# Hybrid decoder layer: the last diagonal key block of each attention unit transposed and split in the bank of the second one, and the steps listed in a new order

## The chip, the cores and the metric

The kernel runs on one core of one Trainium2 chip. The metric is the device time of one execution in microseconds (us), lower is better. Engines are named as in the profile: PE is the matmul engine (PEld its weight loads), DVE the vector engine, ACT the scalar engine, POOL the general engine, SP the engine that issues most of the DMAs.

## The reference

One layer of a decoder works on 1024 rows of width 1024. A gated DeltaNet group and an attention group read the same normalised input; their outputs are projected together and added to the residual, then come an MLP of width 4096, an input embedding added under a gate, and a last norm. The change is in the attention group, which has eight heads and a causal softmax:

```python
def blocked_causal_attention(q, k, v):
    ...
    def block(args):
        q_blk, start = args
        s = jnp.einsum('bhqd,bhkd->bhqk', q_blk, k, preferred_element_type=jnp.float32) * scale
        q_idx = start + jnp.arange(Q_BLOCK)
        s = jnp.where(key_idx[None, :] <= q_idx[:, None], s, -jnp.inf)
        pr = jax.nn.softmax(s, axis=-1).astype(v.dtype)
        return jnp.einsum('bhqk,bhkd->bhqd', pr, v)
...
        y_mla = mla_mixer(c_q, c_kv, k_pe, positions, q_norm_w[i], w_q_b[i], kv_norm_w[i],
                          w_kv_b[i], mla_out_norm_w[i])
        h = h + jnp.concatenate([y_gdn, y_mla], axis=-1) @ w_out[i]
```

## The kernel before, in words

The kernel is one straight program. It is cut into 576 named steps, and a hand-written list, `STEPS`, gives the order in which their code is emitted. A scheduler then puts the instructions of each engine into one fixed order when the program is built; each engine works through its order and waits where an operand or a buffer is not there. SP issues its DMAs in such an order too, so that a DMA which waits for a buffer holds up those behind it.

Matrix operands that need full precision are kept as a rounded part ("hi") and a remainder ("lo"). `evac_split` makes both out of a PSUM bank: ACT casts the bank into hi (L179), then DVE subtracts hi from the bank into lo (L180).

Attention is worked off in 16 units: unit `u` is head `u // 2` and query half `g = u % 2`, that is 512 queries in four blocks of 128 (`i` = 0 to 3). The steps of a unit are:

- `s{u}_{i}` (`scores_block`): scores of one query block in PSUM (tile `ps_s`), the row maximum on DVE (`stat`), the exponential on ACT into `pn`.
- `v{u}_{kb}` (`values_part`): for the key block `kb` of 128 keys, PE transposes the blocks of `pn` (128x128 each) into one PSUM bank `pt_p`, of which there are two; `evac_split` makes `phl` of them; PE multiplies hi and lo with the values `V[..., kb]` and sums into the bank `po_a` (L1124, L1125), of which there is one. On the diagonal, `kb >= 4 * g`, only the query blocks that see the key block take part: key block `4g` has four query blocks (512 columns), `4g + 1` three (384), `4g + 2` two (256) and `4g + 3` one (128). A unit has `4g + 4` key blocks.
- `ve{u}` (`values_end`): ACT and DVE bring `po_a` to `oT` (L1134, L1135); the next unit's first product needs the bank.
- After each pair of heads `fa` and `fb` divide by the softmax sums (`rb`, on POOL or DVE, L1155), write `y_d`, and sum squares with 16 narrow matmuls on PE (`pss`, L1160).

Between them in the list stand steps of other parts: the DeltaNet outputs, head projections (`wn`, `wv1`, `vc`), the embedding (`plew` loads `wp0` and `wp1` and splits them: raw tiles `wp0r`, `wp1r`, halves `wp0h`, `wp1h`; `ei`, `eo` use them), and at the end the output projection: `wo0` to `wo7` load and split eight row blocks of the weight, `y0` to `y7` its input, `pa` (`po`, uses blocks 0 to 3) and `pb` (`po_o`, uses blocks 4 to 7) multiply, `h` loads the residual, `wu` the first weights of the MLP. Raw weights, `wp1r` and `rb` share pools of buffers with other tiles.

Of the kernel before, what the change touches and what calls it, by code (L numbers as in the profile page):

```python
# [64 lines left out]
STEPS = """
ldx0 ldm0 start ldx2 ldx1 ldx7 ldx3 ldm1 mixcol ldm2 nx0 nx1 ldm3 ldx5 tx0_3 nx2 nx3 tx0_7 ldx4 tx0_0 tx0_1 tx1_6
tx0_5 tx0_4 columns tx1_7 tx1_1 spm0 spm2 nx5 tx0_2 masks spm3 tx1_0 spm1 tx0_6 tx1_4 nx7 ldx6 tx1_3 tx1_2 tx1_5
misc2 nx4 nx6 tx2_5 misc0 misc1 tx2_0 la00 tx2_2 tx2_1 wl7 tx2_3 misc3 tx2_7 tx2_4 tx2_6 misc6 wl4 misc5 misc4 misc7
gates ip4 cv4 wl5 ssk0_0 ssk0_1 ip5 dec0 dec1 cv5 wl0 ssk1_1 wl6 ip7 ssk1_0 wl1 ip6 cv7 dec3 wl2 ssk3_0 dec2 cv6
ssk2_1 wl10 ssk2_0 gk1 ssk3_1 cvals ip1 rotary cv1 cunit ip0 gk0 cv0 ssq0_0 ssq0_1 uu1 ip2 gk2 uu2 gk3 uu0 uu3 wl3  # L70
sub sub0 ssq1_1 sub1 la11 sub2 sub3 sub4 sub5 sub6 sub7 sub8 sub9 xout ssq1_0 cv2 ssq2_1 wl8 wl9 ssq2_0 ip3 cv3 wl13
qout0 ip8 la10 cv8 rv0_0 rv0_1 kbd1_0 ga3 ga2 ssq3_0 qout1 wl11 ip9 cv9 kbd3_0 kbd2_0 tl0 kbd0_1 ga1 ga0 tm0 ip11
tn0 ip10 wl12 kbd1_1 rv1_0 tl1 tm1 kbd0_0 mw0 cv10 tl2 tl3 ip12 cv12 tn1 mw1 kbd3_1 kbd2_1 ssq3_1 rv2_0 rv1_1 tm2
tn2 cv11 ip13 cv13 rv3_1 tm3 tn3 mw2 mw3 rv3_0 mu0 sc0 rv2_1 mu3 mu1 wl15 mu2 sc1 sc2 sc3 wl14 ip15 qout2 ip14 cv14
la01 lt0_2 sc4 lt1_1 lt0_0 sc5 cv15 lt0_1 sc6 lt1_0 sc7 sc8 sc9 sc10 wv0 vb1 wpe qp0 vb0 qp1 sc11 vb3 rq8 vb2 lt1_2
rkey sc12 sc13 sc14 qout3 ol6 qp7 qr00 qp2 vb6 wn0 kn0_1 vb5 ol0 vb4 kn0_0 sc15 ol2 ol3 qn0_0 qp4 vb7 ol1 kp3 oa0
qp5 oa1 kp0 ob0 qp6 qp3 qn0_1 qr01 qr11 oa2 ro0_0 s0_1 qr10 s0_2 s0_3 ro0_1 s0_0 v0_0 v0_1 v0_2 s1_2 s1_0 s1_1 v0_3
ve0 s1_3 v1_0 v1_1 v1_2 v1_3 v1_4 kp1 s2_0 v1_5 kp2 v1_6 v1_7 ve1 ob1 ob2 s2_2 oa3 s2_1 ol4 oa4 ob3 s2_3 ob4 s3_1
ol5 s3_0 oa6 v2_0 s3_3 v2_1 v2_2 oa5 ob6 s3_2 v2_3 wn1 qn1_0 ro1_0 qn1_1 kn1_1 ve2 v3_0 v3_1 kn1_0 ro1_1 v3_2 v3_3
v3_4 s4_2 s4_1 fa0 ol7 s4_0 oa7 s5_2 s4_3 v3_5 v3_6 v3_7 ve3 v4_0 v4_1 v4_2 s5_1 fb0 s5_0 s6_2 s5_3 v4_3 ob5 s6_1  # L80
ve4 v5_0 kp5 s7_1 v5_1 v5_2 v5_3 v5_4 v5_5 v5_6 wv1 vc1 s6_3 ob7 ro2_0 s7_2 v5_7 s7_0 vc0 plew ei0 ei1 eo1 eo0 s6_0
h2 ve5 v6_0 v6_1 v6_2 wn2 kn2_0 v6_3 vc4 vc5 vc3 s7_3 vc7 ve6 v7_0 v7_1 v7_2 v7_3 qn2_0 vc6 vc2 v7_4 fa1 ei2 v7_5
qn2_1 kp4 s8_3 kn2_1 s8_1 eo2 ro2_1 v7_6 s8_2 s8_0 kp7 s9_3 s10_3 s9_1 s9_0 v7_7 ve7 v8_0 fb1 v8_1 v8_2 v8_3 s9_2
ve8 v9_0 v9_1 v9_2 v9_3 v9_4 ei3 s10_0 eo3 s10_2 s10_1 s11_1 s11_0 ei4 v9_5 v9_6 v9_7 ro3_0 ve9 s11_2 eo4 v10_0
v10_1 v10_2 v10_3 ve10 s11_3 ei5 ro3_1 eo5 wn3 qn3_0 kn3_0 v11_0 kn3_1 kp6 v11_1 v11_2 v11_3 v11_4 fa2 s12_2 qn3_1
ei6 s12_1 s12_0 v11_5 v11_6 v11_7 ei7 y0 ve11 s12_3 v12_0 v12_1 v12_2 v12_3 s13_3 eo6 ve12 s13_2 s13_1 eo7 fb2 s13_0
v13_0 v13_1 v13_2 s14_1 v13_3 v13_4 y2 v13_5 s14_3 v13_6 v13_7 ve13 s14_2 s14_0 v14_0 v14_1 y1 v14_2 v14_3 ve14 wo0
s15_0 s15_1 h6 s15_3 s15_2 v15_0 wo1 wo2 v15_1 wo3 y4 y5 y3 fa3 v15_2 v15_3 v15_4 v15_5 v15_6 h3 h4 pa4 y6 v15_7
ve15 fb3 wo4 h7 pa3 rsy h0 wo5 h5 wo6 pa0 y7 pa5 pa7 pa6 wo7 h1 wu0 pb3 pa2 pb2 nh2 nh3 pb0 nh0 pb7 pa1 uo0 pb1 nh1 th0_1
pb4 nh7 wu1 pb6 nh6 th0_0 th0_2 nh4 pb5 nh5 th0_3   th1_1 th1_0  th1_2  th1_3    # L90
 
"""
# [1530 lines left out]
```

## Time and profile before

| | |
|---|---|
| median of 3 runs | 1457.66 us (1456.11 to 1465.13) |
| profiled execution | 1459.25 us, span of its trace 1457.5 us |
| busy, share of the span | PE 95%, PEld 78%, DVE 69%, ACT 45%, POOL 21% |
| attention, 412 to 641 us of the trace | 229 us |
| rest of the output projection, 641 to 705 us | 64 us |

A busy share is the time in which an engine works on an instruction. Times in the rows below are microseconds from the start of the span, and the mean of one instruction is in nanoseconds. PEclk is the clock that was granted to PE as a share of its full speed.

### The profile page before, as it was taken

Reading aid. Unit: us, or ns where it says so; the run is one execution under the profiler, and the core shown is the slowest. Engines: PE = TensorE matmul, PEld = TensorE weight load, DVE = VectorE, ACT = ScalarE, POOL = GpSimd, SP = SyncE. Lnnn points to the kernel's source line nnn. Section 1 sums busy time; section 2 is a strip of 40 time slices with the busy share of each in tenths; the row PEclk is TensorE's granted clock in tenths of the full one; section 3 lists DMA queues with packets and bytes.
Section 4 is the critical chain, followed back from the end, with each engine's and each line's share of the span. In section 5 each row is a group of like instructions: output and inputs, shape, how many; then the busy total and the mean of one; then the engine's idle time right before and its main releaser. Section 6 shows DMA issues by size and latency. Waiting matters only on the chain.

```text
span 1457.5 us, 22314 instructions
## 1 busy us (share of the span) xinstructions
PE 1380.4 (95%) x8575; PEld 1130.7 (78%) x8575; DVE 1007.5 (69%) x1617; ACT 662.8 (45%) x1169; POOL 307.4 (21%) x417
## 2 busy tenths in 40 slices
PE   5999968999899999999989999999999999999897
PEld 4877847887677777888767888878887888888786
DVE  5567499545679687764697877778758775765464
ACT  6444210322357788842554544445534333333442
POOL 5412196321243511231510000000000000001410
...
GB/s 214 49 54 59 131 58 130 85 81 86 59 66 65 140 82 106 152 196 130 88 66 151 159 159 159 159 137 125 214 333 230 159 96 126 183 116 134 170 44 58
DMA packets 133590, 182.54 MB, mean 125 GB/s; under 512 B 38896, under 2 KB 88188, under 8 KB 133484
## 3 DMA queue, kind: packets, MB, share of 16 engines
...
q10 hardware_dynamic: 160, 0.27, 0.0%
HBM read 122.99 MB, written 58.10 MB: 124 GB/s over the span
## 4 chain that ended last, share of the span: by engine, by line
PE 47%; DVE 11%; DMA 8%; ACT 6%; issue 3%; POOL 1%; SPq 1%; DVEq 0%; POOLq 0%; ACTq 0%
DMA i_d<-D 4%; PE dmo L214 3%; PE dme L214 3%; PE dmo L215 3%; PE dme L215 3%; PE dme L213 3%; PE dmo L213 3%; DMA dar<-i_d 2%; PE pgt L215 2%; PE pgt L213 2%; PE pgt L214 2%; PE um L215 2%; PE um L214 2%; PE um L213 2%; PE pt_p L1119 1%
## 5 line engine op out<-in xcount | busy, mean ns | idle before, releaser
L1495 DVE TENSOR_TENSOR dal<-dar,dah 128x1024 fp32r<-128x1024 f32 x56 | 68.5, 1224 | 74.4 <-issue 32.1
L1544 POOL DMA_DIRECT2D rowg<-in_ple_gate_norm_w x1 | 0.6, 644 | 505.4 <-DVE dbs L1499 505.4
L214 PE MATMUL dme<-dbl,dah 128*128 128x512 f32 x256 | 99.7, 390 | 0.0
L215 PE MATMUL dme<-dbh,dal 128*128 128x512 f32 x256 | 99.4, 390 | 0.0
L213 PE MATMUL dme<-dbh,dah 128*128 128x512 f32 x256 | 99.2, 390 | 0.0
L1494 ACT CAST dah<-dar 128x1024 fp32r<-128x1024 f32 x56 | 58.8, 1050 | 62.0 <-DMA dar<-i_d 59.5
L1501 ACT CAST dbh<-dbs 128x1024 fp32r<-128x1024 f32 x40 | 42.1, 1053 | 90.1 <-DVE dbs L1499 45.6
L214 PE MATMUL dmo<-dbl,dah 128*128 128x512 f32 x192 | 74.4, 390 | 1.8 <-DVE dbl L1502 1.8
L215 PE MATMUL dmo<-dbh,dal 128*128 128x512 f32 x192 | 74.3, 390 | 0.0
L213 PE MATMUL dmo<-dbh,dah 128*128 128x512 f32 x192 | 72.8, 390 | 0.0
L180 DVE TENSOR_TENSOR phl<-pt_p,phl 128x512 fp32r<-128x512 f32 (+1 forms) x96 | 51.8, 550 | 17.8 <-ACT phl L179 16.8
L1098 DVE TENSOR_REDUCE stat<-ps_s 128x1 f32<-128x384 f32 (+5 forms) x96 | 51.5, 551 | 16.4 <-PE ps_s L1097 9.7
L213 PEld LDWEIGHTS dme<-dbh,dah 128*128 128x128 f32 x256 | 48.1, 188 | 10.0
L214 PEld LDWEIGHTS dme<-dbl,dah 128*128 128x128 f32 x256 | 48.1, 188 | 9.9
L215 PEld LDWEIGHTS dme<-dbh,dal 128*128 128x128 f32 x256 | 48.1, 188 | 9.9
L213 PE MATMUL um<-uc,t52h 128*128 128x512 f32 x128 | 51.4, 402 | 3.5 <-DVE Cb L1420 2.7
L179 ACT CAST phl<-pt_p 128x512 fp32r<-128x512 f32 (+1 forms) x96 | 44.5, 480 | 21.9 <-PE pt_p L1119 19.5
L1502 DVE TENSOR_TENSOR dbl<-dbs,dbh 128x1024 fp32r<-128x1024 f32 x40 | 48.9, 1222 | 6.7 <-ACT dbh L1501 6.4
L214 PE MATMUL um<-uc,t52h 128*128 128x512 f32 x128 | 50.8, 397 | 2.6 <-DVE uc L1282 2.6
L214 PE MATMUL um<-uc,t34h 128*128 128x512 f32 x128 | 50.7, 396 | 0.7 <-DVE uc L1282 0.7
L213 PE MATMUL um<-uc,t34h 128*128 128x512 f32 x128 | 50.9, 398 | 0.0
L215 PE MATMUL um<-uc,t34l 128*128 128x512 f32 x128 | 50.4, 393 | 0.0
...
## 6 DMA issues: line engine op xcount, KB each, us to landing
...
```

The lines of the kernel that those rows point to most:

```text
L179: nc.scalar.copy(out=hi, in_=src)
L180: nc.vector.tensor_tensor(out=lo, in0=src, in1=f(hi), op=ALU.subtract)
L213: nc.tensor.matmul(outp, ah, bh, start=first, stop=False)
L214: nc.tensor.matmul(outp, ah, bl, start=False, stop=False)
L215: nc.tensor.matmul(outp, al, bh, start=False, stop=last)
L1098: nc.vector.tensor_reduce(out=st[:, c:c + 1], in_=ps[c], axis=AX.X, op=ALU.max, negate=True)
L1119: nc.tensor.transpose(pt[:, i * P:(i + 1) * P], pn_view(u, i)[:, kb * P:(kb + 1) * P], ident)
L1494: nc.scalar.copy(out=ah, in_=raw)
L1495: nc.vector.tensor_tensor(out=al, in0=raw, in1=f(ah), op=ALU.subtract)
L1501: nc.scalar.copy(out=bh, in_=s_)
L1502: nc.vector.tensor_tensor(out=bl, in0=s_, in1=f(bh), op=ALU.subtract)
L1544: nc.gpsimd.dma_start(out=rowg, in_=ple_gate_norm_w[0].partition_broadcast(P))
```

## The change: what it does

In `values_part`, the one 128x128 block of the last key block (`kb + 2`, query block 3) is transposed into the bank of the second diagonal key block, ahead of its three. The bank is then 512 columns wide instead of 384, and is cast and subtracted once. After the two products of the second key block (384 columns) follow the two of the last one (128 columns, with its own values, L1141 and L1142). The step of the last key block goes, so that a unit has `4g + 3` value steps, and the third diagonal key block (256 columns) comes last; `ve{u}` waits for that one. PE has the same transposes and products as before; ACT has 16 casts of 128 columns less, DVE 16 subtractions of 128 columns less, and 16 casts and 16 subtractions grow from 384 to 512 columns. `STEPS` is also listed in another order from attention on. In the build the two kernels' engine orders are alike up to the start of attention, and again from the MLP's first product on; between them they differ. Line numbers of after are 9 higher up to the scores, and 17 higher behind `values_part`.

```diff
-ve0 s1_3 v1_0 v1_1 v1_2 v1_3 v1_4 kp1 s2_0 v1_5 kp2 v1_6 v1_7 ve1 ob1 ob2 s2_2 oa3 s2_1 ol4 oa4 ob3 s2_3 ob4 s3_1
...
+s1_0 s1_1 ve0 s1_3 v1_0 v1_1 v1_2 v1_3 v1_4 kp1 s2_0 v1_5 kp2 v1_6 ve1 ob1
...
-        for i in range(i0, 4):
-            nc.tensor.transpose(pt[:, i * P:(i + 1) * P], pn_view(u, i)[:, kb * P:(kb + 1) * P], ident)
-        cs = slice(i0 * P, 512)
+
+        parts = [(kb, i) for i in range(i0, 4)]
+        if i0 == 1:
+            parts.insert(0, (kb + 2, 3))
+        for j, (b, i) in enumerate(parts):
+            nc.tensor.transpose(pt[:, j * P:(j + 1) * P], pn_view(u, i)[:, b * P:(b + 1) * P], ident)
+        n = len(parts) * P
         ph, pl = hl(slot("phl", "phl", F32R))
-        evac_split(pt[:, cs], ph[:, cs], pl[:, cs])
-        vt = V[hh // 4, kb][:, hh % 4 * P:(hh % 4 + 1) * P]
-        nc.tensor.matmul(po[:, cs], vt, ph[:, cs], start=(kb == 0), stop=False)
-        nc.tensor.matmul(po[:, cs], vt, pl[:, cs], start=False, stop=(kb == nkb - 1))
+        evac_split(pt[:, :n], ph[:, :n], pl[:, :n])
+        vt = [V[hh // 4, b][:, hh % 4 * P:(hh % 4 + 1) * P] for b in (kb, kb + 2)[:1 + (i0 == 1)]]
+        cs, m = slice(i0 * P, 512), i0 == 1
+        nc.tensor.matmul(po[:, cs], vt[0], ph[:, m * P:n], start=(kb == 0), stop=False)
+        nc.tensor.matmul(po[:, cs], vt[0], pl[:, m * P:n], start=False, stop=(kb == nkb - 2))
+        if m:
+            nc.tensor.matmul(po[:, 384:512], vt[1], ph[:, 0:P], start=False, stop=False)
+            nc.tensor.matmul(po[:, 384:512], vt[1], pl[:, 0:P], start=False, stop=False)
...
-        for kb in range(4 * g + 4):
-            step(f"v{u}_{kb}", *(f"s{u}_{i}" for i in range(4)), f"v{'bc'[hh // 4]}{kb}", *([f"v{u}_{kb - 1}"] if kb else []),
+        for kb in range(4 * g + 3):
+            step(f"v{u}_{kb}", *(f"s{u}_{i}" for i in range(4)), f"v{'bc'[hh // 4]}{kb}", *([f"v{'bc'[hh // 4]}{kb + 2}"] if kb == 4 * g + 1 else []), *([f"v{u}_{kb - 1}"] if kb else []),
                  *([f"ve{u - 1}"] if u and not kb else []))(lambda u=u, kb=kb: values_part(u, kb))
-        step(f"ve{u}", f"v{u}_{4 * g + 3}")(lambda u=u: values_end(u))
+        step(f"ve{u}", f"v{u}_{4 * g + 2}")(lambda u=u: values_end(u))
```

The first place is PE at the end of unit 1 (head 0, second half), before: the products of its second, third and last diagonal key block; `pav` is DeltaNet work, `pn2a` the next unit.

```order
L1124 MATMUL po_a<-phl,V_3927 128x384
L1119 MATMUL pt_p<-ident,pn_4308 128x128
L1119 MATMUL pt_p<-ident,pn_4366 128x128
L1125 MATMUL po_a<-phl,V_3927 128x384
L1119 MATMUL pt_p<-ident,pn_4366 128x128
L885 MATMUL pav<-Uv_3092,A_3970 64x64 x16
L1124 MATMUL po_a<-phl,V_3899 128x256
L1125 MATMUL po_a<-phl,V_3899 128x256
L1124 MATMUL po_a<-phl,V_3899 128x128
L1119 MATMUL pt_p<-ident,pn2a 128x128 x3
L1125 MATMUL po_a<-phl,V_3899 128x128
```

The same place after:

```order
L1138 MATMUL po_a<-phl,V_3927 128x384
L1132 MATMUL pt_p<-ident,pn_4311 128x128
L1132 MATMUL pt_p<-ident,pn_4362 128x128
L1139 MATMUL po_a<-phl,V_3927 128x384
L1141 MATMUL po_a<-phl,V_3899 128x128
L1142 MATMUL po_a<-phl,V_3899 128x128
L1132 MATMUL pt_p<-ident,pn2a 128x128 x3
L894 MATMUL pav<-Uv_3092,A_3970 64x64 x12
L1138 MATMUL po_a<-phl,V_3899 128x256
L894 MATMUL pav<-Uv_3092,A_3970 64x64 x4
L1139 MATMUL po_a<-phl,V_3899 128x256
```

The narrow products moved ahead of the 256-column ones, and the unit's last product is one bank earlier.

The second place is the load of the embedding weights in the middle of attention. SP before:

```order
L1156 DMA y_d<-oT_4363 128x1024
L198 DMA wp0r<-in_w_ple_proj 128x1024
L198 DMA wp1r<-in_w_ple_proj 128x1024
L906 DMA y_d<-ot_4650 128x4x128
L979 DMA wv1r<-in_w_kv_b 128x4x64
```

SP after:

```order
L988 DMA wv1r<-in_w_kv_b 128x4x64
L207 DMA wp0r<-in_w_ple_proj 128x1024
L1173 DMA y_d<-oT_4359 128x1024
L207 DMA wp1r<-in_w_ple_proj 128x1024
L915 DMA y_d<-ot_4553 128x4x128
```

The loads of `wv1r` and `wp0r` moved ahead of the write of `oT`. On ACT the casts of these weights stand between casts of value blocks, before:

```order
L179 CAST phl<-pt_p 128x512
L192 CAST wp0h<-wp0r 128x1024
L179 CAST phl<-pt_p 128x512
L179 CAST phl<-pt_p 128x384
L192 CAST wp1h<-wp1r 128x1024
L179 CAST phl<-pt_p 128x256
L192 CAST wv_5315<-wv1r 128x256
```

ACT after:

```order
L201 CAST wp0h<-wp0r 128x1024
L188 CAST phl<-pt_p 128x512
L898 ACTIVATE ot_4979<-ot_4979 128x512
L1114 ACTIVATE pn6a,sums_110<-ps_s,stat 128x128
L188 CAST phl<-pt_p 128x512
L1008 CAST V_5266<-pv 128x2x64 x2
L188 CAST phl<-pt_p 128x256
L1047 ACTIVATE qh_5325<-pt_qp 32x512
L1151 COPY oT_5186<-po_a 64x512
L201 CAST wp1h<-wp1r 128x1024
```

The cast of `wp1h` moved behind the unit's last value block and its `oT` copy.

The third place is SP near the end of attention, around the last unit's `oT`. Before:

```order
L198 DMA wo5r<-in_w_out 128x1024
L1269 DMA h_7079<-in_x 128x1024
L1150 DMA rb_6921<-r_d 64x1024 x2
L1269 DMA h_7071<-in_x 128x1024
L198 DMA wo6r<-in_w_out 128x1024
L1231 DMA yr_7003<-y_d 128x1024
L1156 DMA y_d<-oT_6527 128x1024
L1231 DMA yr_7115<-y_d 128x1024
L198 DMA wo7r<-in_w_out 128x1024
L1269 DMA h_7213<-in_x 128x1024
L1351 DMA wu_7215<-in_w_up 128x4x256
L1351 DMA wu_7216<-in_w_up 128x4x256
```

After:

```order
L207 DMA wo6r<-in_w_out 128x1024
L1368 DMA wu_7030<-in_w_up 128x4x256
L1368 DMA wu_7031<-in_w_up 128x4x256
L1167 DMA rb_6853<-r_d 64x1024 x2
L1286 DMA h_6954<-in_x 128x1024
L1248 DMA yr_6956<-y_d 128x1024
L1173 DMA y_d<-oT_6475 128x1024
L1248 DMA yr_7075<-y_d 128x1024
L207 DMA wo7r<-in_w_out 128x1024
L1286 DMA h_7117<-in_x 128x1024
L207 DMA wo5r<-in_w_out 128x1024
```

The load of `wo5r` moved from far ahead of the write of `oT` to behind `wo7r`, and the two loads of `wu` moved ahead of `rb`.

## Rows read from the trace of the kernel before

**Rows 1.** Stretches: bounds, length, busy us and count per engine, PEclk, DMA share, GB/s.

```profile
412.00:641.00 229.00, 218.21 (x1561) 177.16 (x1560) 180.94 (x353) 173.04 (x451) 68.93 (x100) 0.99 0.38 124
...
641.00:705.00 64.00, 64.00 (x295) 53.26 (x294) 33.08 (x46) 17.73 (x26) 12.97 (x15) 1.00 0.25 91
705.00:745.00 40.00, 33.74 (x160) 26.78 (x159) 29.53 (x35) 26.52 (x47) 25.48 (x22) 0.87 0.24 79
```

**Rows 2.** Waits of PE, 412 to 641: waiting, releaser, total, times, longest.

```profile
PE po_a L1124 <- ACT phl L179: 2.2, 3, 1.1
...
PE po_a L1125 <- DVE phl L180: 0.9, 2, 0.7
```

**Rows 3.** Waits of ACT, the same stretch.

```profile
ACT phl L179 <- PE pt_p L1119: 18.6, 16, 5.2
...
ACT oT L1134 <- PE po_a L1125: 3.0, 3, 1.3
```

**Rows 4.** Groups by shape, ACT, 412 to 642: busy us, mean ns, idle before.

```profile
L179 ACT CAST phl<-pt_p 128x512 fp32r<-128x512 f32 x48 | 27.4, 586 | 9.9 <-PE pt_p L1119 9.4
...
L179 ACT CAST phl<-pt_p 128x384 fp32r<-128x384 f32 x16 | 7.7, 482 | 1.7 <-PE pt_p L1119 1.5
...
L179 ACT CAST phl<-pt_p 128x128 fp32r<-128x128 f32 x16 | 4.3, 266 | 1.2 <-PE pt_p L1119 1.2
```

**Rows 5.** Groups by shape, DVE, the same stretch.

```profile
L180 DVE TENSOR_TENSOR phl<-pt_p,phl 128x512 fp32r<-128x512 f32 x48 | 32.6, 682 | 5.5 <-ACT phl L179 4.9
...
L180 DVE TENSOR_TENSOR phl<-pt_p,phl 128x384 fp32r<-128x384 f32 x16 | 8.8, 550 | 2.3 <-ACT phl L179 2.2
...
L180 DVE TENSOR_TENSOR phl<-pt_p,phl 128x128 fp32r<-128x128 f32 x16 | 4.6, 286 | 2.0 <-ACT phl L179 1.7
```

**Rows 6.** Timeline of ACT around 490: start, length, instruction, idle before.

```profile
484.49 1.07 ACT L179 CAST phl<-pt_p 128x512 fp32r<-128x512 f32 x2
...
491.28 1.05 ACT L192 CAST wp0h<-wp0r 128x1024 fp32r<-128x1024 f32 x1 [1.01 <-DMA wp0r<-in_w_ple_proj]
...
494.87 1.04 ACT L192 CAST wp1h<-wp1r 128x1024 fp32r<-128x1024 f32 x1 [1.68 <-DMA wp1r<-in_w_ple_proj]
```

**Rows 7.** Groups by shape, PE, 412 to 642: the 128-column product.

```profile
L1124 PE MATMUL po_a<-phl,V 128*128 128x128 f32 x15 | 4.0, 269 | 0.0
```

**Rows 8.** Timeline of PE around 490.

```profile
492.86 0.49 PE L1124 MATMUL po_a<-phl,V 128*128 128x512 f32 x1 [0.63 <-ACT phl L179]
...
496.23 0.39 PE L1124 MATMUL po_a<-phl,V 128*128 128x256 f32 x1 [1.14 <-ACT phl L179]
```

**Rows 9.** Timeline of SP's DMA issues around 490.

```profile
487.11 0.42 SPq L198 DMA_DIRECT2D wp0r<-in_w_ple_proj  x1
490.08 0.33 SPq L198 DMA_DIRECT2D wp1r<-in_w_ple_proj  x1
```

**Rows 10.** Timeline of PE after the last value product.

```profile
645.53 0.28 PE L1125 MATMUL po_a<-phl,V 128*128 128x128 f32 x1
...
657.75 1.84 PE L1160 MATMUL pss<-ones,rb 128*128 128x1 f32 x16
```

**Rows 11.** Timeline of SP's DMA issues, same place.

```profile
655.46 0.37 SPq L198 DMA_DIRECT2D wo7r<-in_w_out  x1
...
656.40 1.15 SPq L1351 DMA_DIRECT2D wu<-in_w_up  x2
```

**Rows 12.** Timeline of ACT, same place.

```profile
652.36 1.06 ACT L1157 ACTIVATE rb<-oT 128x1024 f32<-128x1024 f32 x1 [4.86 <-POOL oT L1155]
...
660.26 1.05 ACT L192 CAST wo7h<-wo7r 128x1024 fp32r<-128x1024 f32 x1
```

**Rows 13.** Timeline of DVE, same place.

```profile
645.95 1.22 DVE L193 TENSOR_TENSOR wo5l<-wo5r,wo5h 128x1024 fp32r<-128x1024 f32 x1
```

**Rows 14.** Timeline of POOL, same place.

```profile
647.58 2.40 POOL L193 TENSOR_TENSOR wo6l<-wo6r,wo6h 128x1024 fp32r<-128x1024 f32 x1 [19.84 <-ACT wo6h L192]
```

**Rows 15.** Stretch 600 to 605, columns as in Rows 1.

```profile
600.00:605.00 5.00, 5.00 (x25) 4.37 (x25) 2.33 (x7) 3.41 (x10) 2.36 (x1) 0.68 0.47 151
```

More of the change, by code (lines that the diff above doesn't have):

```diff
@@ L65 @@
 STEPS = """
[L66 to L75, printed above, removed]
@@ L76 @@
-rkey sc12 sc13 sc14 qout3 ol6 qp7 qr00 qp2 vb6 wn0 kn0_1 vb5 ol0 vb4 kn0_0 sc15 ol2 ol3 qn0_0 qp4 vb7 ol1 kp3 oa0
-qp5 oa1 kp0 ob0 qp6 qp3 qn0_1 qr01 qr11 oa2 ro0_0 s0_1 qr10 s0_2 s0_3 ro0_1 s0_0 v0_0 v0_1 v0_2 s1_2 s1_0 s1_1 v0_3
-ve0 s1_3 v1_0 v1_1 v1_2 v1_3 v1_4 kp1 s2_0 v1_5 kp2 v1_6 v1_7 ve1 ob1 ob2 s2_2 oa3 s2_1 ol4 oa4 ob3 s2_3 ob4 s3_1
-ol5 s3_0 oa6 v2_0 s3_3 v2_1 v2_2 oa5 ob6 s3_2 v2_3 wn1 qn1_0 ro1_0 qn1_1 kn1_1 ve2 v3_0 v3_1 kn1_0 ro1_1 v3_2 v3_3
-v3_4 s4_2 s4_1 fa0 ol7 s4_0 oa7 s5_2 s4_3 v3_5 v3_6 v3_7 ve3 v4_0 v4_1 v4_2 s5_1 fb0 s5_0 s6_2 s5_3 v4_3 ob5 s6_1
@@ L81 @@
[L81 to L90, printed above, removed]
+ldx0 ldm0 start ldx2 ldx1 ldx7 ldx3 ldm1 mixcol ldm2 nx0 nx1 ldm3 ldx5 tx0_3 nx2
@@ new lines @@
+nx3 tx0_7 ldx4 tx0_0 tx0_1 tx1_6 tx0_5 tx0_4 columns tx1_7 tx1_1 spm0 spm2 nx5 tx0_2 masks
+spm3 tx1_0 spm1 tx0_6 tx1_4 nx7 ldx6 tx1_3 tx1_2 tx1_5 misc2 nx4 nx6 tx2_5 misc0 misc1
+tx2_0 la00 tx2_2 tx2_1 wl7 tx2_3 misc3 tx2_7 tx2_4 tx2_6 misc6 wl4 misc5 misc4 misc7 gates
+ip4 cv4 wl5 ssk0_0 ssk0_1 ip5 dec0 dec1 cv5 wl0 ssk1_1 wl6 ip7 ssk1_0 wl1 ip6
+cv7 dec3 wl2 ssk3_0 dec2 cv6 ssk2_1 wl10 ssk2_0 gk1 ssk3_1 cvals ip1 rotary cv1 cunit
+ip0 gk0 cv0 ssq0_0 ssq0_1 uu1 ip2 gk2 uu2 gk3 uu0 uu3 wl3 sub sub0 ssq1_1
@@ new lines @@
+sub1 la11 sub2 sub3 sub4 sub5 sub6 sub7 sub8 sub9 xout ssq1_0 cv2 ssq2_1 wl8 wl9
+ssq2_0 ip3 cv3 wl13 qout0 ip8 la10 cv8 rv0_0 rv0_1 kbd1_0 ga3 ga2 ssq3_0 qout1 wl11
+ip9 cv9 kbd3_0 kbd2_0 tl0 kbd0_1 ga1 ga0 tm0 ip11 tn0 ip10 wl12 kbd1_1 rv1_0 tl1
+tm1 kbd0_0 mw0 cv10 tl2 tl3 ip12 cv12 tn1 mw1 kbd3_1 kbd2_1 ssq3_1 rv2_0 rv1_1 tm2
+tn2 cv11 ip13 cv13 rv3_1 tm3 tn3 mw2 mw3 rv3_0 mu0 sc0 rv2_1 mu3 mu1 wl15
+mu2 sc1 sc2 sc3 wl14 ip15 qout2 ip14 cv14 la01 lt0_2 sc4 lt1_1 lt0_0 sc5 cv15
+lt0_1 sc6 lt1_0 sc7 sc8 sc9 sc10 wv0 vb1 wpe qp0 vb0 qp1 sc11 vb3 rq8
@@ new lines @@
+vb2 lt1_2 rkey sc12 sc13 sc14 qout3 ol6 qp7 qr00 qp2 vb6 wn0 kn0_1 vb5 ol0
+vb4 kn0_0 sc15 ol2 ol3 qn0_0 qp4 vb7 ol1 kp3 oa0 qp5 oa1 kp0 qp6 ob0
+qp3 qr01 qn0_1 ro0_0 oa2 qr11 s0_1 qr10 s0_2 s0_3 ro0_1 s0_0 v0_0 v0_1 v0_2 s1_2
+s1_0 s1_1 ve0 s1_3 v1_0 v1_1 v1_2 v1_3 v1_4 kp1 s2_0 v1_5 kp2 v1_6 ve1 ob1
+ob2 s2_2 oa3 s2_1 ol4 ol5 oa4 ob3 s2_3 ob4 s3_1 s3_0 v2_0 oa6 s3_3 v2_1
+oa5 ob6 s3_2 wn1 v2_2 kn1_1 ve2 qn1_0 ro1_0 qn1_1 v3_0 v3_1 kn1_0 ro1_1 v3_2 v3_3
+v3_4 s4_2 s4_1 fa0 ol7 s4_0 v3_5 oa7 s5_2 s4_3 v3_6 ve3 s5_1 v4_0 v4_1 v4_2
@@ new lines @@
+fb0 s5_0 s5_3 ob5 ve4 s6_1 s7_1 v5_0 kp5 v5_1 v5_2 wv1 s6_2 vc1 s6_3 v5_3
+v5_4 v5_5 v5_6 ro2_0 s7_2 vc0 plew s7_0 ob7 ei0 ei1 eo1 eo0 ve5 s6_0 v6_0
+v6_1 wn2 kn2_0 h2 vc4 vc5 vc3 s7_3 vc7 v6_2 ve6 v7_0 v7_1 v7_2 v7_3 qn2_0
+vc6 vc2 v7_4 qn2_1 kp4 fa1 ei2 v7_5 s8_3 kn2_1 s8_1 eo2 ro2_1 v7_6 s8_2 s8_0
+kp7 ei5 s9_3 s10_3 s9_1 s9_0 ve7 v8_0 fb1 v8_1 v8_2 s9_2 ve8 v9_0 v9_1 v9_2
+v9_3 v9_4 ei3 s10_1 s11_0 s11_1 ei4 v9_5 v9_6 ro3_0 ve9 s11_2 s10_0 eo3 s10_2 eo4
+v10_0 v10_1 v10_2 s11_3 ve10 eo5 wn3 ro3_1 v11_0 v11_1 qn3_0 kp6 kn3_0 s12_2 qn3_1 v11_2
@@ new lines @@
+kn3_1 v11_3 v11_4 fa2 ei6 s12_1 ei7 y0 v11_5 s12_0 v11_6 ve11 s12_3 v12_0 v12_1 v12_2
+s13_3 eo6 ve12 s13_2 s13_1 eo7 fb2 s13_0 v13_0 v13_1 v13_2 s14_1 v13_3 s14_3 v13_4 s14_0
+y2 v13_5 v13_6 ve13 s14_2 v14_0 y1 v14_1 v14_2 ve14 wo0 s15_0 s15_1 h6 s15_3 s15_2
+wo1 wo2 v15_0 y4 v15_1 wo3 y3 fa3 y5 wo4 v15_2 v15_3 h7 v15_4 h3 h4
+pa4 v15_5 v15_6 h0 y6 pa7 pa6 ve15 h5 wo6 wu0 fb3 pa0 y7 pa5 wo7
+h1 rsy pa3 wo5 pb3 pa2 pb2 pb0 nh2 pa1 nh3 nh0 pb1 pb7 nh1 uo0
+th0_1 pb4 nh7 nh4 wu1 pb6 nh6 th0_0 th0_2 pb5 th0_3 nh5 th1_1 th1_0 th1_2 th1_3
```

## The prediction

> **What bounds the kernel now.** I read the busy time by stretch first. Between 412 and 641 us, which is attention, PE is busy for 218.21 of 229.00 us, DVE for 180.94 (79%) and ACT for 173.04 (76%) [rows 1]. The reader is to see that PE bounds even this stretch, and that 10.8 us is all that PE has there in idle time. From 641 to 705 us PE is busy without a gap, 64.00 of 64.00; from 705 to 745 it lacks 6.3 us [rows 1], in the hand-over to the MLP, whose first products come when the last norms are transposed. Next I read what PE waits for in attention: 2.2 us in three waits for the cast of a value block and 0.9 us in two for its subtraction [rows 2]. The rest of the 10.8 us is split over many small waits for exponentials, projections and `oT`. The other engines wait for PE much longer: ACT waits 18.6 us for transposes before it can cast [rows 3]. So work taken off ACT or DVE is worth what PE waits for it, which is 3.1 us of the 10.8, and not its own length.
>
> **The change, part by part.** PE does the same transposes, products and columns, so its busy time has no term.
>
> *The merge.* For each unit a cast of 384 columns and one of 128 become one of 512: 482 + 266 - 586 = 162 ns less on ACT, by 16 units 2.6 us [rows 4]. The subtractions give 550 + 286 - 682 = 154 ns, 2.5 us on DVE [rows 5]. These are upper ends, because neighbours overlap: two casts of 512 columns take 1.07 us together where twice 586 is 1.17 [rows 6], so a dropped instruction frees some 0.06 to 0.16 us, 0.9 to 2.6 us in all. This lies beside PE's work. On the other side the first product of the merged block waits for a cast that is 104 ns longer (586 - 482) and a subtraction that is 132 ns longer (682 - 550): 0.236 us by 16 is 3.8 us, if PE stood waiting at each of them. The 384-column blocks are hidden now, and so are the 128-column ones, whose first product has an idle time of 0.0 over 15 units [rows 7]; the round trip that goes from the end of each unit was paid by PE nowhere that the profile shows. What can come of it is that ACT's copy of `oT`, which waits 3.0 us for the last product in three places [rows 3], is reached a bank earlier, and that the two busiest helpers are 1% less loaded. Between -2.6 and +3.8 us I take -1.0: it is nearest to the freed time after overlap (0.9), and the lengthening is covered by the product stream in between, as the 0.0 shows.
>
> The profile shows ACT at 76% and DVE at 79%, neither full, with PE waiting for both at times [rows 1, 2]. The Trainium skill (Perfetto Trace Analysis, section Optimizing Scalar/DVE Operations) says that grouping into larger operations helps where the engine is saturated, and that where it isn't and yet causes bubbles on other engines, breaking instructions up may let work finish sooner. By that rule the merge goes the wrong way; the term would be up to +3.8 instead of -1.0. It is the first rival below. The same section puts the fixed cost of an operation on PSUM at about 51 ns on ACT and 125 ns on DVE; by it the merge would free an estimated 0.8 and 2.0 us, inside the span from the rows.
>
> *The order around the embedding weights.* This is where PE's longest waits for a cast are. SP issues `wp0r` at 487.11, behind the write of `oT`, and `wp1r` only at 490.08 [rows 9]. ACT's order has both casts in the middle of value blocks: it stands idle for 1.01 us before `wp0h` and 1.68 before `wp1h` [rows 6], and PE then waits 0.63 us at 492.86 and 1.14 us at 496.23 for casts of value blocks queued behind them [rows 8]. After, `wp0r` is issued ahead of the write, and `wp1h`'s cast stands behind the unit's last block and its `oT` copy. The two waits have no reason left: 1.77 us. I take -2.0, since the subtraction behind a late cast is late too, with ends 0 and -2.7 (1.01 + 1.68, all of ACT's idling). At nothing it stands if the load of `wp1r`, which still waits for a buffer, lands later than the cast's new place; behind that cast is queued the next unit's first value block.
>
> *The rest of the order in attention.* Every score, value and projection step shifts by a few places. The same kinds of work are left, with the same buffers; new small waits replace old ones. PE's idle time without the above two places is about 8.8 us (10.8 - 2.0); one unit end less per round trip takes a little of it. I take -1.0, between -5 and +6. The upper end is some six waits of the longest kind seen (1.14 us) [rows 8].
>
> *The end of attention.* From 641 to 705 us PE never waits [rows 1], so nothing can be won, only lost. Let E be the end of the last value product, 645.53 + 0.28 = 645.8 [rows 10]. Before, POOL did `wo6l` for 2.40 us ahead of the last `oT` [rows 14]; the change casts `wo6h` before that unit ends, and `oT` with all behind it comes 2.4 us sooner after E. Two things run against PE. First, `pss` needs the squares of `oT`: 652.36 + 1.06 - 2.4 = 651.0, E + 5.2 [rows 12]; 43 products stand between E and `pss`, at 64.00 / 295 = 0.217 us each [rows 1], so PE reaches it at E + 9.3. Margin 4.1 us. Second, `wo5r` is now issued two rows behind `wo7r`, where `wu` was: 656.40 - 2.4 = 654.0 [rows 11]. `wo7r` was cast 4.8 us after its issue (660.26 - 655.46) [rows 11, 12], so `wo5r` lands by 658.8. Its cast stands behind `wo7h`: 660.26 + 1.05 - 2.4 = 658.9, end 660.0; its subtraction adds 1.22 [rows 13], 661.2 or E + 15.4. PE meets the first `wo5` product after 79 products and `pss` (1.84) [rows 10]: 79 x 0.217 + 1.84 = 19.0. Margin 3.6 us. I cost both at nothing; the cover is 17 us of products with the first four row blocks, and each microsecond beyond the margin would be one of the time. From 705 to 745 us the orders nearly agree: 0, within 1 us.
>
> *The clock.* The granted clock is 0.99 in attention, but 0.68 from 600 to 605 [rows 15], where PE had just done 16 one-column products. Going without this dip would give 5 x (1 - 0.68) = 1.6 us, one more of them would cost as much; what the new order does to it the rows don't tell. 0, within 1.6.
>
> **The sum.** -1.0 - 2.0 - 1.0 + 0 = -4.0 us. The profiled execution took 1459.25, so 1455.2 by it; it stands 1.6 us above the median of the runs (1457.66), which gives 1453.7, rounded 1454.
>
> **The rivals.**
>
> 1. *The merge delays its products.* If PE has caught up with the casts at the second diagonal key block, it pays the longer cast and subtraction: +3.8, and with the order gains lost (0 for -3.0) 1461.5. For it speaks that PE does wait for `phl` [rows 2], and the rule above; against it that the waits are five in some 110 blocks, two of them behind weight casts and not behind a block's own length.
>
> 2. *The queue before the last `oT` (the slower side).* On SP two loads of `wu` now stand ahead of `rb`, and `oT`, `y_d`, the last `yr`, `wo7r` and `wo5r` all stand behind. If a `wu` load waits for its buffer, they are all late, and PE stands at `pss` or at `wo5` from a delay of 3.6 to 4.1 us on, microsecond for microsecond. A delay of 10 us gives +6: with the rest of the sum 1456, without it 1460; over 1% needs a delay near 20. For it: the order and the buffers shared with `wo` and `y`. Against it: in the trace of before `wu` was issued one row behind `h` at 656.40 without holding [rows 11], and the casts that free raw weights stand well ahead of the unit's last block.
>
> 3. *The round trips were the idle time.* If PE's small waits come mostly from ends of units (the next unit can't sum until `po_a` is copied), sixteen shorter ends take most of 10.8 us: -9, 1449. Against it: idle time of 0.0 at the 128-column products [rows 7].
>
> 4. *Nothing happens.* The 128-column blocks are hidden, the weights' wait moves on to another load, new waits are as long as the old: 1457.5, within 1.
>
> **How the numbers follow.** Forecast 1454 (1450 to 1457): 0.48. Rival 1 (1458 to 1465): 0.14. Rival 2: 0.10, of which 0.04 beyond 1%. Rival 3 (1446 to 1450): 0.12. Rival 4: 0.16, of which a little runs into either side. The range leaves out the far part of rivals 2 and 3 and spans the rest: 1446 to 1463. One per cent, 14.6 us, is about what a measurement of this kernel can tell from no change, and it is more than PE's whole idle time in attention. Faster by over 1% therefore needs all of that and more elsewhere: 0.05. Slower by over 1%: rival 2 far out, and an order that breaks up PE's stream in several units: 0.06. Within: 0.89.
>
> **What would show it.** In the trace of after: 512-column casts of `phl` 64, none of 128; ACT's and DVE's busy time in attention lower by 1 to 3 us each, PE's the same; no wait of PE over 0.5 us behind `wp0h` or `wp1h`; PE still without a gap over the output projection; idle time of PE in attention near 7 us. Wrong would be a wait of PE at the first product of merged blocks in many units, a gap before `pss` or `po_o <- wo5h`, or new waits for `stat` and `pn` that sum to over 4 us.

## The result and the profile after

The changed kernel takes 1469.14 us (median of 20 runs, 1458.91 to 1475.62); the kernel before took 1461.53 in the 20 runs beside it (1456.11 to 1467.36). The ratio is 1.0057, with a 95% interval of 1.0042 to 1.0072: about 8 us slower, less than 1% but clear of the noise. I had forecast 4 us less; on the 1457.66 us that the forecast started from, 1.0057 is 1466.0 us, above the range's end of 1463.

The profiled execution took 1475.62 us, 6.5 above the median of its own runs, so I had a second trace of it made later (1472.5 us, span 1470.8). The same was done for the kernel before (1463.37, span 1461.7). Only what both traces of a kernel show is put down to the kernel.

The stretches of the first trace of after; columns as in [rows 1]:

```profile
412.00:661.00 249.00, 231.53 (x1560) 186.40 (x1559) 182.79 (x338) 174.62 (x438) 71.06 (x101) 0.95 0.36 115
484.00:562.40 78.40, 71.15 (x433) 57.52 (x430) 55.23 (x115) 55.54 (x148) 20.74 (x27) 0.93 0.32 97
562.40:661.00 98.60, 91.42 (x474) 74.75 (x472) 69.14 (x111) 67.79 (x156) 23.37 (x25) 0.93 0.46 161
661.00:731.00 70.00, 70.00 (x331) 58.42 (x330) 34.70 (x48) 23.04 (x37) 17.43 (x22) 1.00 0.27 100
```

The first row answers to the first of [rows 1]: PE's idle time has grown from 10.8 to 17.5 us (249.00 - 231.53), and the granted clock has fallen from 0.99 to 0.95. The second trace of after is milder:

```profile
412.00:656.80 244.80, 231.04 (x1582) 186.56 (x1581) 182.36 (x341) 175.18 (x438) 72.06 (x101) 0.96 0.37 117
```

There the idle time is 13.8 us, and in the second trace of before it is 13.2 (412.00 to 649.50, beginning earlier in the work), so most of the growth in idle time belongs to the first trace alone. DVE and ACT have not got more work: their busy times are 1 to 2 us above those of before, in a window that is 16 to 20 us longer (that of before ends 5 us ahead of its last value product). The last row of the first trace, from the last value product to the first product of the MLP, has PE busy throughout, as before.

The forms of the value blocks answer to [rows 4] and [rows 5]: ACT, then DVE, from the first score to the last value product.

```profile
L188 ACT CAST phl<-pt_p 128x512 fp32r<-128x512 f32 x64 | 36.4, 585 | 16.4 <-PE pt_p L1132 13.8 <-issue 1.1 <-PE pv_n L224 0.9
L188 ACT CAST phl<-pt_p 128x256 fp32r<-128x256 f32 x16 | 6.0, 374 | 7.0 <-PE pt_p L1132 7.0
```

```profile
L189 DVE TENSOR_TENSOR phl<-pt_p,phl 128x512 fp32r<-128x512 f32 x64 | 43.3, 683 | 12.8 <-ACT phl L188 12.5
L189 DVE TENSOR_TENSOR phl<-pt_p,phl 128x256 fp32r<-128x256 f32 x16 | 6.7, 417 | 5.5 <-ACT phl L188 5.5
```

There are 64 blocks of 512 columns and none of 128 or 384: the change does what it says.

Where did the time go? Engine orders differ, so a fixed time doesn't compare the same work. I gave every form of PE instruction the spacing that it usually has at full clock, added these up along PE's order from the first score to the MLP's first product (257 us in every kernel), and cut each trace at 21.4% and 43% of that sum. What a trace takes beyond the sum is lost. PE's granted clock has two levels in these traces, full (2.4 GHz) and half (1.2 GHz); the loss is split by the clock granted where it fell, so that a wait in a half-clock part counts as half clock.

```
from 21.4% to 43% of the work   from:to (us)   length   lost at half clock   lost at full clock
before                          486.1:556.3     70.2          0.0                 14.5
before, second trace            490.6:560.6     70.0          0.0                 14.4
after                           484.1:562.4     78.3          4.8                 17.6
after, second trace             489.6:567.8     78.2          5.2                 17.3
```

The two traces of each kernel agree within 0.2 us: 8 us are lost in this stretch, as much as lies between the medians. How much exactly hangs on what counts as the usual spacing; with the median spacing of each form the same cut gives 71.1 and 71.6 us before and 77.3 and 76.7 after, so 5 to 8 us is what the traces bear out. The stretch reaches from the first sums of squares (`pss`) over the embedding weights and `wv1` to about unit 8. The same stretch in the second traces, of before and then of after, and behind it what follows in the second trace of after:

```profile
490.60:560.60 70.00, 65.12 (x386) 52.46 (x387) 55.26 (x117) 54.57 (x147) 17.11 (x24) 1.00 0.34 109
```

```profile
489.60:567.80 78.20, 70.95 (x427) 57.66 (x426) 55.22 (x114) 55.53 (x148) 20.76 (x27) 0.93 0.31 97
567.80:656.80 89.00, 85.56 (x474) 70.26 (x472) 67.40 (x111) 67.51 (x156) 24.28 (x25) 1.00 0.53 179
```

In the stretch PE is idle for 7.3 us (78.20 - 70.95) against 4.9 before (70.00 - 65.12), and busy for 5.8 us more with the same kinds of products. The 5.8 us are mostly clock: in both traces of after 10.2 us of the stretch stand at half clock, in those of before none, and at half the speed that is an estimated 5 us.

The last row against 562.40 to 661.00 above, 89.00 against 98.60 us for the same instructions, shows that the further loss of the first trace was an accident of that execution.

What PE waits for in the stretch, after (first trace):

```profile
PE pt_p L1132 <- DVE phl L189: 2.9, 4, 1.2
PE ps_s L1102 <- ACT pn10b L1114: 1.3, 1, 1.3
PE po_a L1139 <- DVE phl L189: 0.9, 2, 0.6
PE ps_s L1102 <- ACT pn8a L1114: 0.7, 1, 0.7
PE pe L222 <- ACT pthl L188: 0.5, 1, 0.5
```

The first row is new: transposes that wait until the subtraction has freed one of the two `pt_p` banks. The timeline of PE shows where:

```profile
490.11 1.84 PE L1177 MATMUL pss<-ones,rb 128*128 128x1 f32 x16
...
493.57 0.69 PE L1139 MATMUL po_a<-phl,V 128*128 128x384 f32 x1 [0.65 <-DVE phl L189]
...
499.75 0.30 PE L1132 MATMUL pt_p<-ident,pn6b 128*128 128x128 f32 x1 [1.04 <-DVE phl L189]
...
501.78 0.33 PE L1132 MATMUL pt_p<-ident,pn6a 128*128 128x128 f32 x1 [1.18 <-DVE phl L189]
...
503.27 0.69 PE L222 MATMUL pe<-wp0h,pthl 128*128 128x512 f32 x1 [0.52 <-ACT pthl L188]
503.76 0.63 PE L223 MATMUL pe<-wp0l,pthl 128*128 128x512 f32 x1
...
507.02 0.39 PE L222 MATMUL pe<-wp1h,pthl 128*128 128x512 f32 x1
```

The last two rows show the clock: a product of 512 columns takes 0.63 us at half clock and 0.39 at full clock. In the first trace it falls to a half at 493.2, 503.4 and 551.2 us: behind the sums of squares at 490 and 549 us with their one-column products, and behind the two waits around 500. In the second trace it falls at the same three places of the work (499.3, 509.5 and 557.3 us, with the sums of squares at 495.6 and 554.1). ACT at the wait of 499.75:

```profile
496.75 0.58 ACT L1151 COPY oT<-po_a 64x512 f32<-64x512 f32 x1 [0.69 <-PE po_a L1139]
497.23 1.04 ACT L201 CAST wp1h<-wp1r 128x1024 fp32r<-128x1024 f32 x1
498.30 0.58 ACT L188 CAST phl<-pt_p 128x512 fp32r<-128x512 f32 x1
```

The cast of `wp1h`, moved behind the unit's `oT` copy, now stands ahead of the next unit's first value block.

### The profile page after: what moved, and what is told of

Its sections match the earlier page's. It is cut to its first block, busy times and chain, and to the rows that moved or that the text cites. A ratio compares the mean times of both kernels' runs of the same rounds, so it can differ in the third digit from the quotient of the medians.

```text
span 1473.9 us, 22253 instructions
## 1 busy us (share of the span) xinstructions
PE 1390.0 (94%) x8575; PEld 1136.2 (77%) x8575; DVE 1006.9 (68%) x1601; ACT 662.1 (45%) x1153; POOL 306.8 (21%) x417
## 4 chain that ended last, share of the span: by engine, by line
PE 45%; DVE 12%; DMA 9%; ACT 6%; issue 3%; SPq 1%; POOL 1%; DVEq 0%; POOLq 0%; ACTq 0%
DMA i_d<-D 5%; PE dmo L223 3%; PE dme L222 3%; PE dme L224 3%; PE dmo L224 3%; PE dme L223 3%; PE dmo L222 3%; PE pgt L222 2%; PE pgt L224 2%; PE pgt L223 2%; PE pt_p L1132 1%; DMA dar<-i_d 1%; PE um L224 1%; DVE D L1457 1%; PE um L222 1%
## 5 line engine op out<-in xcount | busy, mean ns | idle before, releaser
L1107 DVE TENSOR_REDUCE stat<-ps_s 128x1 f32<-128x512 f32 (+5 forms) x96 | 51.6, 550 | 16.7 <-PE ps_s L1106 9.6
```

Of the source, the lines that this page charges most:

```text
L1107: nc.vector.tensor_reduce(out=st[:, c:c + 1], in_=ps[c], axis=AX.X, op=ALU.max, negate=True)
```

## The experiments

**First theory, first four runs.** The first trace showed three places of the new order where a late cast or subtraction stands ahead of a value block: the one above; ACT's casts of `y0` near 590 us, which wait for a load; and DVE's subtractions of `y4` near 633 us, ahead of unit 14's `oT`:

```profile
590.57 1.14 ACT L1254 CAST y<-yr 128x512 fp32r<-128x512 f32 x2 [2.79 <-DMA yr<-y_d]
```

```profile
592.03 0.50 PE L1138 MATMUL po_a<-phl,V 128*128 128x256 f32 x1 [1.92 <-ACT phl L188]
...
639.25 0.50 PE L1138 MATMUL po_a<-phl,V 128*128 128x512 f32 x1 [3.01 <-DVE oT L1152]
```

So: the order costs the 8 us, at these places. The rival: the merge does, in every unit.

*The merge alone:* the new code with the old list, less the 16 steps that don't exist any more.

```diff
-s1_2 s1_0 s1_1 v0_3 ve0 s1_3 v1_0 v1_1 v1_2 v1_3 v1_4 kp1 s2_0 v1_5 kp2 v1_6 v1_7 ve1
+s1_2 s1_0 s1_1 ve0 s1_3 v1_0 v1_1 v1_2 v1_3 v1_4 kp1 s2_0 v1_5 kp2 v1_6 ve1
...
```

> The merged bank with the step order of before (the 16 dropped steps left out of it, nothing else moved). Order theory (the loss comes from the new order: a cast or subtraction that waits for a load or for POOL stands ahead of value blocks in three places, and the clock falls behind them): time of before within 3 us, most likely 1 us less, ratio 0.998 to 1.002. Merge theory (each merged bank delays its first product): about 8 us more, ratio near 1.0055, with PE waits for phl in many units.

Measured: ratio 1.0116 (1.0079 to 1.0152), 17 us slower than before.

*The order alone:* the old code with the new list, the step of the last key block put back.

```diff
-s1_0 s1_1 ve0
+s1_0 s1_1 v0_3 ve0
...
```

> The separate banks of before with the step order of the changed kernel (each dropped step put back right behind the step of the third diagonal key block). Order theory: 6 to 10 us over before, ratio 1.004 to 1.007, with the same waits at y0, y4 and after the first pss. Merge theory: time of before within 2 us.

Measured: ratio 1.0097 (1.0060 to 1.0134), 14 us slower.

Each part of the change costs more than both together (for the order alone the intervals overlap a little). Both theories fall: the merge isn't harmless in the old order, and the new order isn't free without the merge; the new list fits the merged code better than the old one does. In the stretch between the marks both lose: 486.5 to 566.1 us for the merge alone, 485.4 to 562.4 for the order alone.

```profile
486.50:566.10 79.60, 70.09 (x419) 56.64 (x417) 55.02 (x111) 55.00 (x145) 20.12 (x26) 0.91 0.30 96
```

```profile
485.40:562.40 77.00, 68.71 (x396) 55.67 (x395) 54.80 (x118) 54.57 (x148) 19.38 (x27) 0.96 0.32 93
```

That is 9.6 and 7 us of their 17 and 14. Behind the stretch, up to the MLP's first product, their traces take 170.2 and 168.7 us, where the two of before take 160.2 and 159.6. Whether that is the order too, one trace each can't tell: the two traces of the changed kernel take 168.6 and 158.9 us there.

*`y0` later:*

```diff
-... ei7 y0 v11_5 s12_0 v11_6 ve11 s12_3 v12_0
+... ei7 v11_5 s12_0 v11_6 ve11 s12_3 y0 v12_0
```

> The changed kernel with the step y0 alone moved behind s12_3: ACT's casts of y0, which waited 2.8 us for a load ahead of unit 11's last value block, then stand behind the next unit's first two blocks. Order theory: the PE waits of 1.9 and 0.6 us near 592 go, and with them the 6.9 us of half clock that follow: 2.5 to 6 us less than the changed kernel, 2 to 6 us over before (ratio 1.002 to 1.004). Merge theory: as the changed kernel, 8 us over before.

Measured: 1.0060 (1.0035 to 1.0086). The wait near 592 is gone from the trace, the time is that of the changed kernel.

*`y4` behind `oT`:*

```diff
-wo1 wo2 v15_0 y4 v15_1 wo3 y3 fa3 y5 wo4
+v15_0 wo1 wo2 v15_1 wo3 y4 y5 y3 fa3 wo4
```

> The changed kernel with the steps around the start of unit 15 in the order of before, so that DVE's subtractions of y4 stand behind the oT addition of unit 14 and not ahead of it. Order theory: the PE wait of 3.0 us near 639 goes, and 3.4 us of half clock behind it: 3 to 5 us less than the changed kernel, 3 to 5 us over before (ratio 1.002 to 1.004). Merge theory: as the changed kernel, 8 us over before.

Measured: 1.0067 (1.0043 to 1.0091). The wait of 3.0 us is gone, nothing is won. The second trace of after explains both experiments: there these waits are 0.44 and 0.63 us. They were large in one execution alone. In both experiments the stretch from 21.4% to 43% is 78.3 us long, as in the changed kernel.

**Second theory: the stretch.** The loss is in the stretch near 490 to 560 us. Is it the cast of `wp1h` in its new place, or the clock that falls behind the one-column products?

*Another buffer for `wp1r`,* so that its load needn't wait for the sums of squares and its cast stands behind the next unit's first value block:

```diff
-'wp1r': 'r',
+'wp1r': 'w',
```

> The changed kernel with the raw weight wp1r in another pool of buffers, so that its load doesn't wait for the sums of squares, and the build puts ACT's cast of wp1h behind the next unit's first value block instead of ahead of it. Theory of the weight's wait (the loss between 485 and 560 us comes from casts held up by wp1h): the PE waits of 1.0 and 1.2 us near 500 go and the half clock behind them, 3 to 5 us less than the changed kernel, ratio to before 1.002 to 1.004. Theory of the clock (the clock falls there because PE does little column work after the one-column products, whatever stands in the casts' order): the half-clock stretch stays, at most 2 us less, ratio 1.0045 to 1.006.

Measured: 1.0116 (1.0092 to 1.0139), slower than the changed kernel. The wait behind `wp1h` shrank, but the one after it is still there, and the stretch takes 79.3 us. PE near 503 us in this run:

```profile
503.32 0.33 PE L1132 MATMUL pt_p<-ident,pn6b 128*128 128x128 f32 x1 [0.30 <-DVE phl L189]
...
505.94 0.48 PE L1132 MATMUL pt_p<-ident,pn6a 128*128 128x128 f32 x1 [1.17 <-DVE phl L189]
```

So shortening the wait behind `wp1h` doesn't bring the stretch back. The test is not a clean one: PE's order differs from that of the changed kernel from about 504 us on, in the stretch and behind it, and this run loses time behind it too (165.9 us up to the MLP's first product).

*Wide sums of squares:*

```diff
-ones = ctile("ones", [P, 1])
+ones = ctile("ones", [P, 64])
...
-nc.tensor.matmul(pss[:, b:b + 1], rb[:, b * P:(b + 1) * P], ones, start=True, stop=True)
+nc.tensor.matmul(pss[:, b * 64:(b + 1) * 64], rb[:, b * P:(b + 1) * P], ones, start=True, stop=True)
```

> The changed kernel with the sums of squares multiplied by 64 columns of ones instead of one (the same sums, 64 times; only the first column of each is read), so that PE does more column work there. Theory of the clock: of the stretches of half clock that begin 2 to 7 us behind these products (near 493, 551, 609 us) most go: 3 to 6 us less than the changed kernel, ratio to before 1.0015 to 1.0035. Theory of the weight's wait: the half clock stays, as the changed kernel or 1 to 2 us more, ratio 1.0055 to 1.007.

Measured: 1.0035 (1.0014 to 1.0056), against 1.0057 of the changed kernel: about 3 us less, with the intervals overlapping a little. The products and the stretch (483.8 to 559.4 us) in its trace:

```profile
489.64 1.89 PE L1177 MATMUL pss<-ones,rb 128*128 128x64 f32 x16
```

```profile
483.80:559.40 75.60, 67.66 (x429) 54.82 (x426) 55.09 (x114) 55.50 (x148) 20.79 (x27) 0.98 0.32 100
```

PE's order is that of the changed kernel but for these products. They cost 0.05 us more (1.89 against 1.84). From 421 us on (ahead of it every trace has a fall around the start of attention) the two traces of after have 23.9 and 10.2 us at half clock, in falls of 3.4 or 6.8 us; here one of 3.4 is left, behind the two waits that are still there. The stretch is 2.7 us shorter than in the changed kernel and still 5.5 longer than before. PE is busy in it for 67.66 us instead of 70.95, and idle for 7.9 instead of 7.3: what went is clock, and the waits stayed. Of the 8 us, then, some 5 are clock (10.2 us at half clock, of which this edit took away two thirds) and most of the rest is idle time.

All traces together bear out the part of the one-column products. In the 14 traces that have them the clock falls within 4 us of their start at 24 of the 42 places in attention; in the three traces with 64 columns at none of nine. And the surrounding counts: behind the first sums of squares it falls in all nine such traces whose first half (units 0 to 7) has the merge or the new list, and in none of the five others.

*The same in the kernel before* (the edit as above):

> The kernel before with the same 64 columns of ones. Theory of the clock: the one stretch of half clock in attention, near 602 us behind the third of these products, goes, 1 to 2 us less than before, ratio 0.9985 to 1.0. Theory of the weight's wait: no gain, 0 to 2 us more.

Measured: 1.0000 (0.9979 to 1.0021). Nothing to win there: the second trace of before doesn't have the fall near 602 us at all, and the first has no other behind these products.

*The changed kernel once more:*

> The changed kernel once more, unchanged, for a second trace: what both traces of it show between 485 and 660 us belongs to the order, what one shows alone is an accident of that execution. Both theories: the waits near 500 and 592 and a clock loss of 4 us or more between 485 and 560 again; the 3.0 us wait near 639, behind DVE's slow subtraction, may be there or not.

As told above: the stretch again (78.2 us), the waits near 592 and 639 small.

**Which units.** *The merge in units 8 to 15 alone, old list:*

```diff
-        if i0 == 1:
+        if i0 == 1 and u >= 8:
```

> The step order of before, with the merged bank in units 8 to 15 alone; the build's orders are those of before up to about 545 us. Theory of the stretch (the cost comes from the part between about 485 and 560 us, units 5 to 8, where the first sums of squares, wv1 and the embedding weights lie, and from any change that shifts it): within 3 us of before, ratio 0.998 to 1.002, with 70 us from 486 on for the same work and no half clock there. Theory of the units (every merged unit costs about 1 us, as 17 us for 16 units in the old order): about 8 us over before, ratio 1.004 to 1.007.

Measured: 1.0028 (0.9996 to 1.0059), between the two theories; the stretch 68.9 us, at full clock. What is lost, if anything, lies behind it.

```profile
489.20:558.10 68.90, 64.31 (x390) 52.52 (x386) 54.04 (x115) 54.24 (x148) 18.53 (x26) 1.00 0.34 111
```

*The merge in units 0 to 7 alone, old list* (`u < 8` in the same place):

> The step order of before, with the merged bank in units 0 to 7 alone. Theory of the stretch: most of what the merge costs in the old order, 8 to 17 us over before, ratio 1.006 to 1.012, with half clock between 485 and 560. Theory of the units: about 8 us over, ratio 1.004 to 1.007, spread over the units.

Measured: 1.0079 (1.0054 to 1.0105); the stretch 78.7 us, with the clock at 0.93:

```profile
482.10:560.80 78.70, 69.20 (x416) 55.81 (x415) 54.77 (x112) 55.12 (x146) 20.13 (x26) 0.93 0.31 97
```

*One step of before moved by two places:*

```diff
-v5_7 s7_0 vc0 plew ei0
+v5_7 vc0 plew s7_0 ei0
```

> The kernel before, no merge, with one step moved two places: the score block s7_0 behind plew instead of ahead of vc0, inside the stretch. Theory of the stretch, in its strong form (the old order is tuned so closely there that any shift brings waits and half clock): 3 to 8 us over before, ratio 1.002 to 1.006. Theory of the units, and the weak form of the other: within 2 us of before.

Measured: 1.0036 (1.0011 to 1.0061): 5 us for one score block, between 2 and 9 by the interval. The stretch takes 73.3 us, 3.2 more, all at full clock; PE is busy as before and idle for 8.3 us (73.30 - 65.00):

```profile
492.90:566.20 73.30, 65.00 (x387) 52.32 (x386) 54.71 (x115) 53.90 (x146) 17.89 (x26) 1.00 0.31 97
```

*The kernel before once more:*

> The kernel before once more, unchanged, for a second trace. Theory of the stretch: again about 70 us for the work from 486 on and no half clock in it. If half clock stands there now, the trace of before was a lucky one and the clock is no difference between the kernels.

The stretch takes 70.00 us, without half clock (its row stands in the first section).

**Split at unit 8.** The decisive pair: one half of attention with the list and code of before, the other with those of after.

*Before up to unit 7, changed from unit 8 on.* The list is that of before as far as `v8_0`, then what is left of the list after, in its order; the merge has the condition

```diff
-        if i0 == 1:
+        if i0 == 1 and u >= 8:
```

> Step order and separate banks of before up to unit 7, new order and merged banks from unit 8 on; every engine's order is that of before up to about 545 us. Theory of the stretch: within 2 us of before, ratio 0.9985 to 1.0015; 70 us for the work from 486 on. Theory of both halves: 4 us over or more, ratio above 1.0025.

Measured: 0.9996 (0.9971 to 1.0021). PE's order is that of before up to about 535 us and that of the changed kernel from about 558 us on. The stretch, 489.2 to 560.8:

```profile
489.20:560.80 71.60, 67.04 (x396) 54.40 (x396) 55.96 (x119) 55.03 (x148) 17.56 (x25) 0.98 0.34 107
```

*The same with wide sums of squares:*

> The same with 64 columns of ones in the sums of squares. Theory of the stretch: as the run without them or 1 to 2 us less, ratio 0.997 to 1.001, little half clock in attention. If what is lost in the second half is half clock, this run is faster than the one without by 3 us or more.

Measured: 0.9966 (0.9941 to 0.9992), median 1454.94 us against 1461.80 of before: faster than both kernels, by an interval that ends close to 1. It is 4 to 6 us less than the run without (ratio and median, 1460.76), more than expected. The trace of the run without has two falls behind 421 us, at 549 and 590, 6.8 us at half clock in all; this one has none. The stretch:

```profile
489.70:560.10 70.40, 65.44 (x400) 53.38 (x396) 55.24 (x118) 55.09 (x149) 18.86 (x27) 1.00 0.35 109
```

*Changed up to unit 7, before from unit 8 on* (the lists the other way round, `u < 8`):

> New order and merged banks up to unit 7, step order and separate banks of before from unit 8 on; every engine's order is that of the changed kernel up to about 555 us. Theory of the stretch: the whole loss, 6 to 10 us over before, ratio 1.004 to 1.007, with 78 us for the work from 486 on. Theory of both halves: about 4 us over, ratio 1.002 to 1.0035.

Measured: 1.0088 (1.0057 to 1.0120), above the 1.004 to 1.007 expected. The stretch:

```profile
488.60:565.50 76.90, 70.92 (x419) 58.21 (x418) 54.22 (x112) 54.42 (x147) 20.28 (x26) 0.89 0.31 98
```

The second half of the change, behind the first half of before, costs nothing; a changed first half costs as much as the whole change or more. Where the last run lost its time is less clear: its trace takes 7 us more in the stretch, and 168.4 us behind it up to the MLP's first product, some 9 more than before. The list is that of before there, but the order that the build made of it is not; and it is one trace.

## Why the prediction was wrong, point by point

**What bounds the kernel** was read rightly: PE, with 10.8 us of idle time in attention. The step that failed is the term for the rest of the order: -1.0, bounded at "-5 to +6" by six waits of the longest kind, on the ground that the same kinds of work are left and new small waits replace old ones. The runs showed +8 us for the whole change, 5 to 8 of them in the stretch from 21.4% to 43%: some 5 us of clock (10.2 us at half clock, none before) and 2.4 us of idle time (7.3 against 4.9). The clock stood in a term of its own, at 0.

**The rest of the order** was mis-sized the most: -1.0 where the order alone showed +14 us, the merge in the old order +17, and one moved step +5.

**The merge.** The freed time came as worked out: the value casts on ACT sum to 42.4 us (36.4 + 6.0) where [rows 4], with 6.0 for the 256-column ones, sum to 45.4; DVE's subtractions to 50.0 where [rows 5], with 6.7 for 256 columns, sum to 52.7. That is 3.0 and 2.7 us against 2.6 and 2.5. The prediction says that this lies beside PE's work, and yet takes 0.9 us of it as won; no run shows that gain. What the term lacked is that a dropped instruction moves everything behind it: the merge alone, in the old list, cost 17 us, where my upper end was +3.8 for later first products. In the stretch PE waits for `phl` mostly at transposes that need a bank (2.9 us in four waits) and only 0.9 us at products, so the price wasn't paid where rival 1 saw it. The Trainium skill (Perfetto Trace Analysis, section Optimizing Scalar/DVE Operations), which I weighed in the prediction, names a gain from grouping where the engine is saturated, and from breaking up where it is not and causes bubbles on other engines. The sign came out that way; but the split at unit 8, with eight merged units, came out at 0.9996, so the rule alone doesn't explain it.

**The embedding weights.** "The two waits have no reason left" was a wrong step too. The waits of [rows 8] are gone from their place, and 1.04 and 1.18 us stand a unit further on, the first behind the cast of `wp1h`: the block that I named as queued behind it, and then cost at nothing. So 1.77 us of waits became 2.22, with a fall of the clock behind them, where I had taken -2.0. Moving that cast alone doesn't mend it, as far as the run with the other buffer shows.

**The end of attention** was right: PE without a gap in 70.00 us, no wait before `pss` or the first product of `wo5`. My margins held. From the MLP's first product to the end the two traces of after take 742.9 and 744.1 us, those of before 741.1 and 741.5: 1.4 to 3 us that no term had, and that no run explains.

**The clock** was cost at 0 within 1.6. From 421 us to the last value product 23.9 and 10.2 us stand at half clock in the two traces of after, 3.4 and none in those of before. The wide sums of squares left 3.4, and the median fell by some 3 us: (10.2 - 3.4) / 2 is 3.4. I had seen one such fall behind one-column products [rows 15], and reasoned that the rows can't tell what a new order does; three such products in a new surrounding were three chances, and my bound took in one.

**The rivals.** Rival 2, the slower side, did not happen at its place. Its times were also summed wrongly: 1457.66 + 6 is 1463.7, and with the other gains 1459.7, not 1460 and 1456. The "some 110 blocks" of rival 1 are 96 (48 and three times 16 casts). Of rival 4 the wait of the weights did move on. Slower the kernel was, by order; the range ended at 1463, since I gave the order one bound from the longest waits seen. That the time would lie within 1% held: 1.0057. Of the signs that I named, the casts came (64 and none); the idle time, 13.8 to 17.5 us where I wrote near 7, and the wait of 1.04 us behind `wp1h` did not come as forecast.

What stays open: why the clock falls behind the first sums of squares when the first half is changed and holds when it is not, and where the 2.4 us of idle time come from, of which the listed waits make up some 1.5. The marks compare sums of usual spacings and not the same instructions (427 against some 390). Why the old order with separate banks keeps PE fed there isn't settled, only that it does and that the departures tried here don't.
